# Seven block products for eight in both products of a channel mixing, in two passes through DRAM

## The chip, the cores and the metric

One core of a Trainium2 chip runs the whole program. The metric is the device time of one execution in microseconds (us); the number given for a kernel is the median of several executions. A profile is one further execution with the hardware profiler on; its span runs from the first to the last instruction.

## What is computed

One layer of a decoder trunk, on 2048 prompt tokens and 8 sample tokens, with model width 1024 and float32 inputs and outputs. Token mixing (pooling, gated delta rule and convolution heads) ends in an output projection and a residual, which gives x1. Channel mixing follows. The lines of the reference that matter here are

```
h = rmsnorm(x1) * (1 + scale2) + shift2          # (tokens, 1024)
a = square(relu(h @ w_ff1))                      # w_ff1 (1024, 4096)
x2 = x1 + gate2 * (a @ w_ff2)                    # w_ff2 (4096, 1024)
y = rmsnorm(x2) * g_final
```

in shortened names. The change touches only these lines and the final norm, and leaves token mixing alone.

## The kernel before

All products are made at float32 accuracy out of the faster fp32r format: an operand is kept as a pair, hi (the operand rounded to fp32r, by a cast on ACT) and lo (the operand less hi, by a subtraction in `split_lo`, L125, in channel mixing always on DVE). A product is three matmuls into one PSUM bank: hi by hi, hi by lo, lo by hi. `unit_mm` (L148 to L157) does this for a tile of 128 weight columns over the 8 slices of the 1024 channels.

Token mixing is the program's first part, and its last instructions on PE are the output projection (L156, `ps_ip`), on DVE the residual (L1108, L1109), and on SP the store of x1 to DRAM (L1111, `x_scr`).

Channel mixing (from L1337) runs in two groups of 8 token tiles, the 8 samples being extra columns of the second group. For each group the rows of x1 are loaded (`ff_load`), scaled (L1389), transposed, given scale and shift and split into pairs of 1024 or 1032 columns (`ff_act`, `ff_rows`; PE L184, ACT L189, DVE L193 and L125). Then a loop goes over the 32 tiles of 128 hidden channels:

- `ff1(ft)` loads 128 columns of w_ff1 (`load_unit`, L136) and 128 rows of w_ff2 (L1416), splits both, makes the first product (L156, `ps_f`, blocks of 512 columns in the first group and of 344 in the second), and forms the squared ReLU as a pair: ACT L1423 (ReLU out of PSUM) and L1429 (square), DVE L1430 and L1431.
- `ff2(b, res)` takes a pair of hidden tiles, makes the second product of all 8 token tiles by 2 halves of 512 columns (L1460, 6 matmuls into one bank) and adds it to a sum held in SBUF (DVE L1473; for the first pair ACT L1471).
- For the samples the second product is a small fp32 product (L1441, `ps_smp`, 8 matmuls for a pair of hidden tiles, and DVE L1446).

The first group ends in `finish` (L1487 ff.: gate on POOL, L1496; second residual and final norm on DVE, L1497 and L1501). The second ends in `finish_last` (POOL L1507 and L1526, DVE L1508, L1523, L1524 and L1535, ACT L1533), which takes the last two pairs of hidden tiles product by product. The intermediate, 2048 tokens by 4096 hidden channels, never leaves SBUF.

No table by hand sets the order. The program is written in the order above, and a scheduler in the Tile framework lays out one in-order instruction list for each engine (PE, DVE, ACT, POOL, and SP, which issues the DMAs), from its own estimate of times, from priorities, and from the pools: a tile can be written only when the tile that had its buffer before has been read by all its readers.

## Time and profile before

| | |
|---|---|
| median of 3 runs | 2618.52 us (2617.0 to 2619.83) |
| profiled execution: span | 2612.9 us, mean granted TensorE clock 0.987 |
| median of the runs less that span | 5.6 us |
| busy share of the span | PE 96%, DVE 65%, ACT 36%, POOL 14% |
| DMA | 253.66 MB moved, mean 97 GB/s |

The profiled execution is listed by its span alone; the time of a run also takes in what lies around the span, and that is put at the 5.6 us of the table. Busy is the time in which an engine worked at something. PE's matmuls are pipelined, so that the mean duration of a single one is longer than the distance from one start to the next; the distance is what counts. The chain that ended last is followed back from the last instruction, at each step to what released it.

### The profile page before, as it was taken

Reading aid. Unit: us, or ns where it says so; the run is one execution under the profiler, and the core shown is the slowest. Engines: PE = TensorE matmul, PEld = TensorE weight load, DVE = VectorE, ACT = ScalarE, POOL = GpSimd, SP = SyncE. Lnnn points to the kernel's source line nnn. Section 1 sums busy time; section 2 is a strip of 40 time slices with the busy share of each in tenths; the row PEclk is TensorE's granted clock in tenths of the full one; section 3 lists DMA queues with packets and bytes.
Section 4 is the critical chain, followed back from the end, with each engine's and each line's share of the span. In section 5 each row is a group of like instructions: output and inputs, shape, how many; then the busy total and the mean of one; then the engine's idle time right before and its main releaser. Section 6 shows DMA issues by size and latency. Waiting matters only on the chain.

```text
span 2612.9 us, 35642 instructions
## 1 busy us (share of the span) xinstructions
PE 2512.9 (96%) x13789; PEld 2087.7 (80%) x13789; DVE 1690.0 (65%) x3107; ACT 938.3 (36%) x2021; POOL 355.8 (14%) x257
## 2 busy tenths in 40 slices
PE   7989999989999999999999999999999999999997
PEld 4667777777889788778888888888888888888885
DVE  4978988999898777644444444445854544444458
ACT  3366367348347442552121121212632122121223
POOL 2111212112112235300000000001300000000034
PEclk9999999999999999999999999999999999999998
DMA  8743223323422568741111111112421111111112
GB/s 300 229 142 111 85 77 110 93 81 98 124 87 78 153 213 260 247 140 54 44 49 49 49 49 46 47 37 65 162 81 49 41 50 48 41 49 41 54 43 107
DMA packets 292569, 253.66 MB, mean 97 GB/s; under 512 B 29706, under 2 KB 243403, under 8 KB 292376
## 3 DMA queue, kind: packets, MB, share of 16 engines
q1 hardware_dynamic: 168208, 185.19, 21.9%
q10 hardware_dynamic: 122720, 61.87, 8.5%
q0 software_dynamic: 1472, 4.33, 0.5%
q8 instruction: 108, 1.77, 0.3%
q14 instruction: 61, 0.50, 0.1%
HBM read 218.19 MB, written 33.54 MB: 96 GB/s over the span
## 4 chain that ended last, share of the span: by engine, by line
PE 71%; DVE 18%; DMA 5%; ACT 3%; issue 2%; SPq 0%; POOL 0%; ACTq 0%; DVEq 0%
PE ps_f L156 27%; PE ps_f L1460 26%; PE ps_ip L156 10%; DVE dc L528 4%; DVE wlo L125 2%; DVE cacc L404 2%; PE ps_mod L283 1%; ACT whi L144 1%; DMA g_scr<-ba 1%; PE ps_ip L1163 1%; PE ps_h L184 1%; DMA mraw<-in_w_ada 1%; PE ps_smp L1441 1%; PE ps_pw L501 1%; DMA xt<-x_scr 0%
## 5 line engine op out<-in xcount | busy, mean ns | idle before, releaser
L1460 PE MATMUL ps_f<-w2h,aa 128*128 128x512 f32 x2048 | 654.0, 395 | 0.0
L1473 DVE TENSOR_TENSOR acc<-ps_f,acc 128x512 f32<-128x512 f32 x432 | 298.3, 690 | 264.1 <-PE ps_f L1460 264.1
L1460 PEld LDWEIGHTS ps_f<-w2h,aa 128*128 128x128 f32 x2048 | 384.2, 188 | 96.6 <-issue 6.2
L156 PE MATMUL ps_f<-fhi,whi 128*128 128x344 f32 (+1 forms) x1280 | 449.0, 351 | 1.6 <-ACT fhi L189 0.4
L156 PE MATMUL ps_f<-flo,whi 128*128 128x344 f32 (+1 forms) x1280 | 448.1, 350 | 0.1
L156 PE MATMUL ps_f<-fhi,wlo 128*128 128x344 f32 (+1 forms) x1280 | 446.8, 349 | 0.1
L156 PE MATMUL ps_ip<-hhi,whi 128*128 128x512 f32 (+1 forms) x1112 | 412.7, 372 | 10.0 <-ACT whi L144 4.9
L156 PE MATMUL ps_ip<-hlo,whi 128*128 128x512 f32 (+1 forms) x1112 | 409.6, 369 | 3.9 <-POOL hlo L125 2.8
L156 PE MATMUL ps_ip<-hhi,wlo 128*128 128x512 f32 (+1 forms) x1112 | 409.5, 369 | 1.5 <-DVE wlo L125 1.0
L1460 PE MATMUL ps_f<-w2l,aa 128*128 128x512 f32 x1024 | 404.3, 395 | 0.0
L144 ACT CAST whi<-raw 128x1024 fp32r<-128x1024 f32 x184 | 192.5, 1046 | 336.1 <-PE ps_f L156 194.6
L125 DVE TENSOR_TENSOR wlo<-raw,whi 128x1024 fp32r<-128x1024 f32 x145 | 188.6, 1300 | 128.9 <-ACT whi L144 126.0
L156 PEld LDWEIGHTS ps_f<-fhi,whi 128*128 128x128 f32 x1280 | 240.7, 188 | 32.3 <-issue 5.8
L1433 ACT CAST w2h<-raw 128x1024 fp32r<-128x1024 f32 x64 | 64.4, 1046 | 562.5 <-PE ps_f L1460 553.7
L156 PEld LDWEIGHTS ps_f<-flo,whi 128*128 128x128 f32 x1280 | 240.7, 188 | 24.0 <-DVE flo L125 0.5
L156 PEld LDWEIGHTS ps_f<-fhi,wlo 128*128 128x128 f32 x1280 | 240.3, 188 | 23.5 <-DVE wlo L125 0.3
L156 PEld LDWEIGHTS ps_ip<-hhi,whi 128*128 128x128 f32 x1112 | 212.7, 191 | 52.6 <-ACT whi L144 8.1
L1430 DVE TENSOR_TENSOR sq<-sq 128x344 f32<-128x344 f32 (+1 forms) x160 | 94.5, 591 | 239.2 <-ACT aa L1429 239.0
L156 PEld LDWEIGHTS ps_ip<-hlo,whi 128*128 128x128 f32 x1112 | 212.6, 191 | 39.2 <-POOL hlo L125 4.0
L156 PEld LDWEIGHTS ps_ip<-hhi,wlo 128*128 128x128 f32 x1112 | 212.6, 191 | 37.3 <-issue 3.0
L1460 PEld LDWEIGHTS ps_f<-w2l,aa 128*128 128x128 f32 x1024 | 192.6, 188 | 43.7
L528 DVE SCALAR_TENSOR_TENSOR dc<-glu,dww,dc 128x512 f32<-128x512 f32 x240 | 199.0, 853 | 2.0
(441 smaller groups left out, 2979.5 us busy)
## 6 DMA issues: line engine op xcount, KB each, us to landing
raw<-in_w_ff SPq DMA_DIRECT2D x128, 512.0 KB
raw<-in_w_in ACTq DMA_DIRECT2D x86, 512.0 KB
mraw<-in_w_ada SPq DMA_DIRECT2D x48, 512.0 KB
raw<-y_scr ACTq DMA_DIRECT2D x32, 512.0 KB
xt<-x_scr SPq DMA_DIRECT2D x32, 512.0 KB
xt<-in_x_prompt SPq DMA_DIRECT2D x16, 512.0 KB
xres<-in_x_prompt SPq DMA_DIRECT2D x32, 256.0 KB
x_scr<-xres SPq DMA_DIRECT2D x32, 256.0 KB
```

Source lines behind the costliest of these rows:

```text
L125: eng.tensor_tensor(out=lo, in0=full, in1=hi, op=ALU.subtract)
L144: nc.scalar.copy(out=hi, in_=raw)
L156: nc.tensor.matmul(out=ps, lhsT=a[:, k, :], rhs=b, start=(i == 0), stop=(i == 3 * KT - 1))
L184: nc.tensor.transpose(ps[:, j, :], xt[:, k * P:(k + 1) * P], ident)
L283: nc.tensor.matmul(out=ps[32 * q:32 * q + 32], lhsT=cT[:, k + i, :], rhs=raw[:, i, :], start=(k + i < 4), stop=(k + i >= 4))
L404: nc.vector.scalar_tensor_tensor(out=acc[:, 0:GT], in0=raw[:, j:j + GT], scalar=cw[:, i, j:j + 1], in1=acc[:, 0:GT], op0=ALU.mult, op1=ALU ...
L501: nc.tensor.matmul(out=ps[:, 0:n], lhsT=pww[:, t, mt * P:(mt + 1) * P], rhs=dc[t][:, 0:n], start=(t == 0), stop=(t == 1))
L528: nc.vector.scalar_tensor_tensor(out=d, in0=gt[:, j:j + GT], scalar=dww[:, t, j:j + 1], in1=d, op0=ALU.mult, op1=ALU.add)
L1430: nc.vector.tensor_tensor(out=q, in0=q, in1=q, op=ALU.mult)
L1433: nc.scalar.copy(out=wh, in_=raw)
L1460: nc.tensor.matmul(out=ps, lhsT=a, rhs=w, start=(i == 0), stop=(i == len(terms) - 1))
L1473: nc.vector.tensor_tensor(out=dst, in0=pv, in1=dst, op=ALU.add)
```

## The change

Both products are cut into 2 by 2 blocks, and the eight block products are made as seven, in Winograd's form of Strassen's algorithm: four sums of blocks of the left operand (S1 to S4), four of the right one (T1 to T4), seven products, and sums of these. The sums of operands are made in float32, and each of the seven operands on either side is then split into its hi and lo pair, so a block product is still three matmuls.

Pass 1 (L1590 ff. of the new file) makes the first product and stores its result. For each half of the tokens (`gi`) the normed rows become 28 operand pairs (`x_ops`; 4 channel slices by 7), which fill 28 buffers of 128 by 2 by 512 (`xb` and `xa`). Then 16 pairs of hidden tiles follow. For each, `w1_ops` loads two tiles of w_ff1 and makes 7 operand pairs (4 sums on POOL, 7 casts on ACT, 7 subtractions on DVE); `unit` makes 84 matmuls into 4 banks and joins them by an ACT copy, an ACT ReLU and 5 DVE additions out of PSUM; the first and the last pair of a half use `unit_by_k`, with 7 banks and a loop over the channel slices outside. `a_ops` forms the squared ReLU (one product on POOL, 3 fused instructions on DVE), the four sums of the second product's left operand (POOL), the 7 pairs (ACT and DVE), and stores them in DRAM (`a_scr`, 7 stores of 512 KB, in pieces of 1 KB). The operands of the second half of the tokens are begun during the first (`x_later`, after pairs 3 and 6, by way of DRAM). The samples' first product is now 16 small fp32 matmuls for a pair of hidden tiles (`sample_unit`).

Pass 2 makes the second product: 8 times (`nb`) two pairs of hidden tiles (`q` 0 and 1), and in each 8 steps of two token tiles. `w2_ops` loads two tiles of w_ff2, multiplies them by the gate (POOL, 128 by 1024), makes the sums (4 on POOL) and the 7 pairs. `a_load` brings 1.83 MB of `a_scr` for each step. `block` makes 42 matmuls and adds them to sums that begin as x1 (ACT copy, 6 DVE additions out of PSUM, 3 POOL additions). In the last `nb` each step ends in the final norm (`final`). w_ff2 is read once, where it was read once for each group.

The core of the diff, additions only, with all of `group`, `ff1`, `ff2`, `finish` and `finish_last` removed:

```
+XB = 12
+AO = 4
+WE = 4
+TB = 8
...
+        def split(entry, full):
+            A.copy(out=entry[:, 0, :], in_=full)
+            sub(V, entry[:, 1, :], full, entry[:, 0, :])
...
+        def left_sums(a11, a12, a21, a22, tmp):
+            s1, s2, s3, s4 = (tmp(f"s{i}") for i in range(1, 5))
+            add(Q, s1, a21, a22)
+            sub(Q, s2, s1, a11)
+            sub(Q, s3, a11, a21)
+            sub(Q, s4, a12, s2)
+            return {A11: a11, A12: a12, A22: a22, S1: s1, S2: s2, S3: s3, S4: s4}
+
+        def right_ops(b11, b12, b21, b22, place):
...
+            put(B11, b11)
+            sub(Q, b11, b12, b11)
+            put(B22, b22)
+            sub(Q, b12, b22, b12)
+            sub(Q, b22, b22, b11)
+            put(T2, b22)
+            put(B21, b21)
+            put(T1, b11)
+            put(T3, b12)
+            sub(Q, b21, b21, b22)
+            put(T4, b21)
...
+        def unit(w, x):
+
+            b = {n: bank("ps_" + n) for n in "xyvz"}
+            got = {}
+            for n, ((l, r), name, first, last) in enumerate(PRODUCTS):
+                for j in range(4):
+                    terms(b[name], w[l], x[j][r], j, first and j == 0, last and j == 3)
...
+        def a_ops(gi, p, c):
+
+            Q.tensor_tensor(out=c[0], in0=c[0], in1=c[0], op=ALU.mult)
+            for i in (2, 1, 3):
+                V.scalar_tensor_tensor(out=c[i], in0=c[i], scalar=0.0, in1=c[i], op0=ALU.max, op1=ALU.mult)
+            ops = left_sums(c[0], c[2], c[1], c[3], tmp)
+            for o in LEFT_ORDER:
+                e = ao.tile([P, 4, 2, P], F32R, tag="a", name="ae")
+                full = ops[o].rearrange("p (j t) -> p j t", j=4)
+                A.copy(out=e[:, :, 0, :], in_=full)
+                sub(V, e[:, :, 1, :], full, e[:, :, 0, :])
+                nc.sync.dma_start(out=a_scr[gi][p][:, :, o, :], in_=e.bitcast(F32).rearrange("p j a t -> p j (a t)"))
...
+        RING2 = [(r2, "o")] * 4 + [(ao, "a")] * AO + [(wp, "whi"), (wp, "wlo")] * 2 + [(we, "e")] * WE
...
+            for i in range(2):
+                raw = wp.tile([P, D], F32, tag="raw", name="raw2")
+                nc.sync.dma_start(out=raw, in_=w_ff2[(2 * p + i) * P:(2 * p + i + 1) * P, :])
+                raws.append(raw)
...
+                for raw in raws:
+                    Q.tensor_tensor(out=raw, in0=raw, in1=g2, op=ALU.mult)
+                return right_ops(*(raw[:, s] for raw in raws for s in halves), lambda o: entry(RING2))
...
+            if (gi, j) == tiles[0] and nb + 1 < NB:
+                w_next = [w2_ops(KB * (nb + 1) + q) for q in range(KB)]
+            if (gi, j) == tiles[-1]:
+                w = w_next
+            block(gi, j, w_now, a_now)
```

`V`, `A` and `Q` are DVE, ACT and POOL. The pool `wp` has 2 buffers for `raw`, and RING2 has 16 places, of which one `nb` holds 14.

Three places show how the order moves. The first is POOL in the loop over hidden tiles. Before, its only work there is a small copy for each tile of the second group; in the first group it has nothing between the `a` memset and the sums of `finish`:

```order
L125 TENSOR_TENSOR wlo<-raw,whi 128x1024
L1356 MEMSET a_11373 128x64
L1496 TENSOR_TENSOR acc_11569<-acc_11569,g_11371 128x512 x2
L1496 TENSOR_TENSOR acc_11570<-acc_11570,g_11371 128x512 x2
L1496 TENSOR_TENSOR acc_11571<-acc_11571,g_11371 128x512 x2
```

Now one pair of hidden tiles in pass 1 gives it nine (c is the square, the first four s are the left operand of the second product, the last four those of a later pair's w_ff1):

```order
L1563 TENSOR_TENSOR c_12130<-c_12130 128x512
L1375 TENSOR_TENSOR s_12176<-c_12157,t_12116 128x512
L1378 TENSOR_TENSOR s_12177<-s_12176,c_12130 128x512
L1378 TENSOR_TENSOR s_12178<-c_12130,c_12157 128x512
L1378 TENSOR_TENSOR s_12179<-u_12102,s_12177 128x512
L1375 TENSOR_TENSOR s_12216<-raw 128x512
L1378 TENSOR_TENSOR s_12217<-s_12216,raw 128x512
L1378 TENSOR_TENSOR s_12218<-raw 128x512
L1378 TENSOR_TENSOR s_12219<-raw,s_12217 128x512
```

The nine recur in this order for every pair.

The second place is DVE in the same loop, the end of one pair's list (ae are pairs on the way to `a_scr`, wo pairs of w_ff1; u, c and t hold the sums of products):

```order
L1375 TENSOR_TENSOR c_12157<-ps_v,u_12102 128x512
L1378 TENSOR_TENSOR ae<-c_12130,ae 128x4x128
L1378 TENSOR_TENSOR wo<-raw,wo 128x512
L1565 SCALAR_TENSOR_TENSOR c_12157<-c_12157 128x512
L1375 TENSOR_TENSOR u_12102<-ps_z,u_12102 128x512
L1378 TENSOR_TENSOR wo<-raw,wo 128x512
L1565 SCALAR_TENSOR_TENSOR u_12102<-u_12102 128x512
L1378 TENSOR_TENSOR ae<-s_12177,ae 128x4x128
L1378 TENSOR_TENSOR ae<-s_12176,ae 128x4x128
L1378 TENSOR_TENSOR ae<-u_12102,ae 128x4x128
```

A pair has 22 DVE instructions, 5 of them with an input in PSUM (L1375), 17 with both inputs in SBUF (14 of L1378, 3 of L1565). Before, the matching stretch had the additions out of PSUM of L1473 and the pairs of L125, L1430 and L1431.

The third place is SP where pass 2 goes from one `nb` to the next; `raw_18060` and `raw_18062` are the two w_ff2 tiles of the second pair (`q` 1), `raw_18654` begins the pairs of the `nb` after:

```order
L1663 DMA ai<-a_scr_2_11376 128x768
L1663 DMA ai<-a_scr_3_11377 128x768
L1663 DMA ai<-a_scr_2_11376 128x1024
L1642 DMA raw_18060<-in_w_ff 128x1024
L1663 DMA ai<-a_scr_3_11377 128x1024
L1663 DMA ai<-a_scr_2_11376 128x768
L1663 DMA ai<-a_scr_3_11377 128x768
L1663 DMA ai<-a_scr_2_11376 128x1024
L1663 DMA ai<-a_scr_3_11377 128x1024
L1642 DMA raw_18062<-in_w_ff 128x1024
L1642 DMA raw_18654<-in_w_ff 128x1024
```

The load of `raw_18062` comes behind four loads for the second step of the new `nb`, which take the buffers that the last step of the old one reads. Before, the loads of w_ff2 (L1416) and w_ff1 (L136) alternated on SP with nothing else.

## Rows read from the trace of the kernel before

**Rows 1.** The span in 40 equal slices: busy tenths of the engines, and what the DMA moved.

```profile
PE   7989999989999999999999999999999999999997
...
DVE  4978988999898777644444444445854544444458
...
POOL 2111212112112235300000000001300000000034
...
GB/s 300 229 142 111 85 77 110 93 81 98 124 87 78 153 213 260 247 140 54 44 49 49 49 49 46 47 37 65 162 81 49 41 50 48 41 49 41 54 43 107
```

**Rows 2.** Busy time by stretch: length, PE, PEld, DVE, ACT, POOL (instructions), granted clock, DMA share, GB/s.

```profile
1125.00:1850.00 725.00, 725.00 (x3157) 587.96 (x3156) 344.19 (x476) 174.32 (x245) 25.75 (x18) 1.00 0.18 56
1850.00:2613.00 763.00, 742.45 (x4085) 652.42 (x4083) 410.40 (x729) 194.16 (x356) 63.45 (x59) 0.99 0.19 63
1000.00:1060.00 60.00, 54.72 (x307) 41.29 (x306) 45.14 (x73) 17.75 (x42) 41.19 (x28) 0.98 0.91 288
```

**Rows 3.** The chain that ended last, in order of time, at channel mixing's start: start, us, what.

```profile
1099.55 5.34 DMA xt<-x_scr
...
1106.99 1.06 ACT xt L1389
...
1122.83 1.84 DMA x_scr<-xres
1124.67 22.52 PE ps_f L156 x96
```

**Rows 4.** The same chain where the second group begins.

```profile
1850.69 1.76 PE ps_h L184 x16
...
1857.21 3.50 DMA xt<-x_scr
...
1863.30 1.20 DVE xt L1497 x2
...
1868.80 18.09 PE ps_f L156 x113
1886.89 0.57 PE ps_smp L1441 x8
...
1919.15 11.55 PE ps_f L156 x72
```

**Rows 5.** Groups of PE matmuls in channel mixing: shapes xcount, busy us, mean ns, idle before.

```profile
L1460 PE MATMUL ps_f<-w2h,aa 128*128 128x512 f32 x2048 | 654.0, 395 | 0.0
L1460 PE MATMUL ps_f<-w2l,aa 128*128 128x512 f32 x1024 | 404.3, 395 | 0.0
```

**Rows 6.** PE in order of time, the last matmul of the program.

```profile
2593.61 0.39 PE L1460 MATMUL ps_f<-w2h,aa 128*128 128x512 f32 x1
```

**Rows 7.** POOL and DVE in order of time, in token mixing's last stretch.

```profile
1095.91 2.64 POOL L125 TENSOR_TENSOR wlo<-raw,whi 128x1024 fp32r<-128x1024 f32 x1 [18.13 <-ACT whi L144]
...
1096.22 2.88 DVE L1109 TENSOR_TENSOR xres<-xres,gated 128x512 f32<-128x512 f32 x1
```

**Rows 8.** Groups of POOL instructions in the whole span.

```profile
L1496 POOL TENSOR_TENSOR acc<-acc,g 128x512 f32<-128x512 f32 x16 | 25.5, 1621 | 693.6 <-DVE acc L1495 693.6
...
L1507 POOL TENSOR_TENSOR acc<-acc,g 128x1024 f32<-128x1024 f32 x8 | 20.1, 2515 | 12.8 <-DVE acc L1473 12.8
...
L847 POOL TENSOR_TENSOR q<-q,fr_y 128x512 f32<-128x512 f32 x16 | 19.7, 1253 | 69.2 <-DVE fr_y L117 42.6 <-DVE xs_y L117 15.0 <-ACT halo_q L402 11.6
```

**Rows 9.** Groups of DVE and ACT instructions in channel mixing.

```profile
L1473 DVE TENSOR_TENSOR acc<-ps_f,acc 128x512 f32<-128x512 f32 x432 | 298.3, 690 | 264.1 <-PE ps_f L1460 264.1
...
L1431 DVE TENSOR_TENSOR aa<-sq,aa 128x512 fp32r<-128x512 f32 x64 | 45.1, 705 | 1.6
...
L1501 DVE SCALAR_TENSOR_TENSOR xt<-xt,nr_y,gf 128x512 f32<-128x512 f32 x16 | 11.2, 743 | 0.0
...
L1495 DVE TENSOR_TENSOR acc<-ps_f,acc 128x512 f32<-128x512 f32 x16 | 10.6, 679 | 0.7 <-PE ps_f L1460 0.7
...
L1471 ACT COPY acc<-ps_f 128x512 f32<-128x512 f32 x32 | 18.2, 587 | 15.3 <-PE ps_f L1460 15.3
```

More of the change, by code (lines that the diff above doesn't have):

```diff
@@ L1338, in hybrid_trunk @@
     wq[0] = nc.sync
[L1339 to L1340 removed]
     NF = DFF // P
[L1342 to L1357 removed]
+    NP = NF // 2
@@ new lines, in hybrid_trunk, with w2_ops @@
+        halves = (slice(0, 512), slice(512, 1024))
+        ph3.close()
+        r2 = ph2.enter_context(tc.tile_pool(name="r2", bufs=4))
+        ai = ph2.enter_context(tc.tile_pool(name="ai", bufs=2 * KB))
+        RING2 = [(r2, "o")] * 4 + [(ao, "a")] * AO + [(wp, "whi"), (wp, "wlo")] * 2 + [(we, "e")] * WE
+        ring[0] = 0
+        def w2_ops(p):
+            raws = []
+            for i in range(2):
+                raw = wp.tile([P, D], F32, tag="raw", name="raw2")
+                nc.sync.dma_start(out=raw, in_=w_ff2[(2 * p + i) * P:(2 * p + i + 1) * P, :])
+                raws.append(raw)
+            Q.tensor_copy(out=a32[:, p % 2, :, 0:NS], in_=a_s[:, 2 * p:2 * p + 2, :])
+            ps = bank("ps_s3", psa)[:, 0:256]
+            for j in range(4):
+                for i in range(2):
+                    nc.tensor.matmul(out=ps[32 * j:32 * j + 32], lhsT=a32[:, p % 2, i, :], rhs=raws[i][:, 256 * j:256 * j + 256],
+                                     start=(i == 0), stop=(i == 1))
+            if p == 0:
+                A.copy(out=chunks, in_=ps)
+            else:
+                add(V, chunks, ps, chunks)
+            with tc.high_priority(offset=HP):
+                for raw in raws:
+                    Q.tensor_tensor(out=raw, in0=raw, in1=g2, op=ALU.mult)
+                return right_ops(*(raw[:, s] for raw in raws for s in halves), lambda o: entry(RING2))
@@ new lines, in a_load, with x1_load @@
+        def a_load(gi, j, p):
+            tiles = []
+            for o, n in ((0, 4), (4, 3)):
+                e = ai.tile([P, n, 2, P], F32R, tag=f"i{n}", name="ai")
+                nc.sync.dma_start(out=e.bitcast(F32).rearrange("p o a t -> p o (a t)"), in_=a_scr[gi][p][:, j, o:o + n, :])
+                tiles.append(e)
+            return tiles
+        acc = {}
+        def x1_load(gi, j):
+            for th in range(2):
+                t = 8 * gi + 4 * th + j
+                acc[t] = xa.tile([P, D], F32, tag="x", name="acc")
+                load_rows(x1_scr[t * P:(t + 1) * P, :], P, acc[t])
@@ new lines, in block @@
+        def block(gi, j, w, a):
+            b = {n: bank("ps_" + n) for n in "xyvz"}
+            t1, t2 = 8 * gi + j, 8 * gi + 4 + j
+            c11, c12, c21, c22 = acc[t1][:, halves[0]], acc[t1][:, halves[1]], acc[t2][:, halves[0]], acc[t2][:, halves[1]]
+            for n, ((l, r), name, first, last) in enumerate(PRODUCTS):
+                ps = b[name]
+                for q in range(KB):
+                    at_ = a[q][l // 4][:, l % 4]
+                    for i, (x, y) in enumerate(PAIRS):
+                        nc.tensor.matmul(out=ps, lhsT=at_[:, x, :], rhs=w[q][r][:, y, :],
+                                         start=first and q == 0 and i == 0, stop=last and q == KB - 1 and i == 2,
+                                         skip_group_check=True)
+                if n == 0:
+                    s = tmp("s")
+                    A.copy(out=s, in_=ps)
+                elif n == 1:
+                    u2 = tmp("u2")
+                    add(V, u2, ps, s)
+                    add(Q, c12, c12, u2)
+                    add(Q, c21, c21, u2)
+                elif n == 2:
+                    add(V, s, ps, u2)
+                    add(Q, c22, c22, s)
+                elif n == 3:
+                    add(V, c11, ps, c11)
+                elif n == 4:
+                    add(V, c22, ps, c22)
+                elif n == 5:
+                    add(V, c12, ps, c12)
+                else:
+                    add(V, c21, ps, c21)
@@ L1584 @@
     from concourse.bass_utils import run_bass_kernel_spmd
-    nc = bacc.Bacc("TRN2", target_bir_lowering=False, num_devices=1)
+    nc = bacc.Bacc("TRN2", target_bir_lowering=False, num_devices=1, dynamic_dma_scratch_size=2048)
     arrays, args = {}, []
```

444 lines of the change are left out of this document (243 added, 201 removed).

## The prediction, made before the changed kernel was run

> **What bounds the kernel now.** I read the span in slices first [rows 1]: PE is at nine tenths in nearly every slice, and in the channel mixing (from about slice 18) DVE stands at four to five tenths, POOL at nothing but for the change of groups and the end, and the DMA moves some 50 GB/s. The busy times by stretch say the same [rows 2]: 725.00 of 725 us of PE up to 1850, 742.45 of 763 after it, at a granted clock of 1.00 and 0.99. So PE's matmuls set the time there, and every other engine has room. The chain of waits gives the pace [rows 3, 4]: 96 matmuls of 512 columns in 22.52 us, 72 of 344 in 11.55. One matmul's record is 0.39 us long [rows 6], about 0.16 more than the distance of two starts, so the distance is (22.52-0.16)/96 = 0.233 us, and 0.158 for 344 columns. The same chain shows where the channel mixing begins on PE (1124.67, [rows 3]), the program's last matmul ends at 2594.0 [rows 6], and 18.9 us of norm follow.
>
> **What goes.** The first product has 1536 matmuls of 512 columns and 2304 of 344, the second 2048 + 1024 [rows 5] of 512: 1536 x 0.233 + 2304 x 0.158 + 3072 x 0.233 = 1438 us. The change makes 2688 of 512 for each product, 5376 x 0.233 = 1253 us. PE is relieved of 185 us. The samples' 32 groups of 0.57 us in the second product [rows 4] stay, 18 us. If PE stayed the bound and nothing waited, the end would come about 185 us earlier. The question is how much of it the new work of DVE, POOL and the queues takes back.
>
> **DVE against POOL, the largest term.** Until now POOL hardly works beside DVE. Where it does, the trace shows what happens [rows 7]: a POOL subtraction runs from 1095.91 to 1098.55; a DVE addition with both inputs in SBUF starts at 1096.22 and is done only at 1099.10, 0.55 us after POOL's end. Alone, such DVE instructions take 0.60 us each back to back (two in 1.20, [rows 4]). It works the other way as well: POOL's 512-column product takes 1253 ns in one place and 1621 in the stretch where DVE works between [rows 8]. DVE additions with an input in PSUM, in that same stretch, stay at 679 ns, as everywhere else at 690 [rows 9]. So the two take turns, save for DVE's additions out of PSUM.
>
> A pair of hidden tiles in pass 1 has 9 POOL instructions and 17 of DVE with both inputs in SBUF. In turns they take 9 x 1.253 = 11.3, plus 9 x 0.55 behind POOL, plus 8 x 0.60 behind DVE, together 21.0 us. PE's 84 matmuls take 19.6. So PE is no longer the bound there. DVE works in order: near a pair's end four stores' subtractions (the ae rows) stand behind the last fused square, which waits for PE's last product, and two of the POOL sums for these. I add 1.3 us for what of that hole the five additions out of PSUM don't fill, and take 22.3 us. Ends: 19.6 (the turns hidden) and 21.0 + 5 x 0.68 = 24.4 (nothing of the additions hidden). 32 x 22.3 = 714 us. ACT has some 16 instructions of 0.59 [rows 9], 9.4 us, and is hidden.
>
> The Trainium skill, page "SBUF — State Buffer", section "Who interferes with whom", speaks against this change: a VectorE instruction with two SBUF inputs contends with a GpSimd instruction that reads SBUF, whoever is first keeps the port for the whole instruction, and the other is fully blocked, while one SBUF input doesn't contend. The trace agrees (0.55 us after POOL's end; 679 ns undisturbed). By that rule a pair costs 21.0 us at least, without it 19.6: 45 us over 32 pairs.
>
> **The stages of pass 1.** Making 28 pairs of the normed rows takes 16 POOL sums and 28 DVE subtractions, in turns 16 x 1.253 + 28 x 0.60 = 36.8 us. At the start, the second four row tiles are loaded only behind the last store of x1, which lands at 1124.67 [rows 3]: 5.3 us for loads in a row and 1.1 for the scale [rows 3], then 36.8, then the last fourth of PE's first unit (4.9), less the 22.3 that this pair has in the sum already: 26 us (10 to 40). At the change of halves the 28 buffers come free a fourth at a time during the last unit; three fourths of 36.8 and 4.9 lie open: 33 us (15 to 45). `x_later` adds 64 transposes at 0.11 [rows 4], 7 us. The sample products of pass 1 are on PE, which has 2.7 us to spare in each pair: nothing; without that cover 16 x 18 small matmuls of at most 0.07 (8 in 0.57, [rows 4]), 20 us.
>
> **To pass 2.** Its buffers take the place of those of the x operands, so the first loads wait for the last unit: 1.83 MB at 288 GB/s, the best stretch seen [rows 2], 6.4 us, then two POOL products of 2.5 [rows 8], two sums of 1.25, cast and subtraction 1.2, of which only some overlap: 15 us. The nearest stall of this kind, at the change of groups, is 11.6 us from load to the next run of matmuls [rows 4]; ends 8 and 25.
>
> **Pass 2.** 2688 x 0.233 = 626 us and 18 for samples. A step takes PE 9.8 us; its 6 DVE additions (4.1), 3 POOL sums (3.8, in no turn with these) and 1.83 MB of loads (6.4) lie beside it: nothing; without that cover a step would be the sum of a load and its products. At each of the 7 changes of `nb` there is something open. Of 16 ring places 14 are held, and `raw` has 2 buffers, so the second pair's tiles are loaded only when the first pair is split, which waits for the old step's last products. On SP `raw_18062` stands behind four loads that wait for the same step. It lands at 2.35 MB/288 = 8.1 us (alone 3.5, [rows 4]); two products, two sums, cast and subtraction make its T2 ready at 16.8. Meanwhile PE has 33 matmuls of the first pair and the samples, 8.3. Open: 8.5 us each, 60 us (27 with the load alone; 98 at 14 each, if the first pair's five late splits come in turns with POOL too). On POOL the steps' sums queue behind the gate products, on DVE behind the late splits; PE then has 5 banks for 4 in use.
>
> The last `nb` adds 4 fused products of 0.74 [rows 9] and a short chain for every step; its 9.6 us on DVE about fill the step: 4 us (0 to 8). After the last matmul one addition, square sums, the chain, four products and a store (1.84, [rows 3]) make 10 us in place of 18.9.
>
> **Sum.** 1124.7 + 714 + 26 + 33 + 7 + 15 + 626 + 18 + 60 + 4 + 10 = 2638 us of span, against 2612.9: 25 us more. What lies around the span is 5.6 us by the median of the runs, so 2643 us: **slower by about 1%**. By parts: 185 of matmuls, about 13 of the old change of groups (1469 less 1438 and 18) and 9 of the tail go; pass 1's turns bring 87, its stages 66, pass 2's changes 79.
>
> **Rivals.**
> - *The turns don't bind* (faster): DVE and POOL meet less than I think, and PE sets pass 1. Then 32 x 19.6 = 627 with 20 for samples; the start falls to 12, the change to 16 (20 us of POOL sums in place of 36.8 in turns); the sum is 1124.7 + 647 + 12 + 16 + 7 + 15 + 626 + 18 + 60 + 4 + 10 = 2540, time 2545. For it: my 21.0 is near 19.6, and the additions out of PSUM fit under POOL. Against: rows 7 and 8. It decides from 21.5 us for a pair: 0.8 us less in each of 32 undoes the 25 us.
> - *The changes of `nb` run in series* (slower): 17 us in place of 8.5 at each of the 7, when the five late splits hold up ACT and DVE and no bank is free for the first pair's work: 60 more, 2703. For it: the SP order. Against: PE's order has work of the first pair ahead of the second's.
> - *The stores bind*: 3.67 MB stored and 1.05 loaded in 22.3 us is 212 GB/s, against 288 seen [rows 2], and four buffers for seven stores of 3.5 us [rows 4] pass in 8 us. Only at under three fourths of the rate seen does this bind; at half of it a pair would take 33 us and the time be some 340 us longer. The Trainium skill, page "Perfetto Trace Analysis", section "DMA Optimizations", warns of transfers under 2 KB, and the stores are in pieces of 1 KB; no row here times such stores by themselves.
> - *It doesn't do what it says*: the lists of instructions hold 84 matmuls for a pair in place of 96, so no.
>
> **How the numbers follow.** A measurement of this kernel can tell about 0.2%, 5 us, from no change. The forecast, from 2600 to 2690, gets 0.46; the first rival, 2500 to 2600, 0.35; the second, over 2690, 0.16; the third 0.03. Of the forecast's part 0.06 lies below 2613 and 0.05 within 5 us of no change. So faster 0.41, same 0.05, slower 0.54. The range goes from 2540, just under the first rival's time, to 2740, the second rival's 2703 with the upper ends of start, change of halves and change of passes on top (14 + 12 + 10); about 1 in 10 is left out at either end.
>
> **What would show it.** Pass 1: PE busy about 85 to 90% of the stretch, the distance of two pairs 22 us, DVE's ae and wo subtractions with a mean well over 0.7 us, POOL's sums over 1.25, the squares and sums of DVE out of PSUM still 0.68. A distance of 19.6 and a PE strip of nines makes the first rival right. Pass 2: seven gaps of PE of 6 to 11 us, each ended by a w_ff2 pair, and none in the steps between. PE's matmul time must fall by 185 us; if it doesn't, the clock was lower or the pace not 0.233, and the whole sum is wrong.

## The result, and the profile after

The changed kernel takes 2831.94 us (median of 4 runs, 2829.26 to 2839.94) against 2619.18: a ratio of 1.081, 95% interval 1.080 to 1.083. It is slower by 8.1%, where about 1% was forecast and the range ended at 2740. The profiled execution spans 2827.3 us, 214 more than before and 190 more than the sum's 2638.

The page of the changed kernel, busy time and the strips that answer to [rows 1], with the busy time of before ahead of it:

```profile
PE 2512.9 (96%) x13789; PEld 2087.7 (80%) x13789; DVE 1690.0 (65%) x3107; ACT 938.3 (36%) x2021; POOL 355.8 (14%) x257
```
```profile
PE 2480.7 (88%) x12797; PEld 1925.3 (68%) x12797; DVE 2094.4 (74%) x3369; ACT 1027.7 (36%) x2252; POOL 1199.1 (42%) x808
...
PE   7989998999999997799898799995888978978976
...
DVE  4988998999987766699899899995444544544467
...
POOL 2111221222122362556566666563654554555442
PEclk9999999999999999899999899997999988988978
...
GB/s 301 228 112 104 96 78 99 95 90 120 91 78 156 223 263 186 77 230 252 245 219 187 164 212 206 202 200 334 139 167 171 171 145 168 176 160 155 201 124 167
```

PE's nines are broken from slice 16 on. In pass 1 (slices 16 to 27) DVE stands at eight to nine for most of it and POOL at five to six; in pass 2 no engine is full, and PE's strip goes up and down. PE's busy time fell by 32 us where the sum took 185 of matmuls away: that is one of the prediction's own signs of being wrong, and a lower clock is one of the two reasons that it names for it. The pattern of pass 2 is one that no term of the sum had at this size. The busy times by stage, to be read with [rows 2] (length, PE, PEld, DVE, ACT, POOL, clock, DMA share, GB/s), say how much:

```profile
1125.00:1935.00 810.00, 711.70 (x3363) 548.69 (x3364) 712.76 (x797) 342.29 (x598) 488.33 (x313) 0.94 0.63 203
1935.00:2070.00 135.00, 93.67 (x386) 67.97 (x384) 68.05 (x84) 21.71 (x37) 71.69 (x50) 0.82 0.62 219
2070.00:2680.00 610.00, 537.49 (x2210) 397.27 (x2209) 290.45 (x386) 78.38 (x132) 320.57 (x227) 0.91 0.48 166
2680.00:2827.00 147.00, 97.60 (x352) 68.87 (x352) 94.55 (x200) 31.49 (x83) 43.97 (x31) 0.84 0.44 154
```

The rows are pass 1, the boundary with the first `nb`, six `nb` in the middle, and the last with the end. Set against the sum, stage by stage (us). An `nb` is counted from its first product to the next one's; by the sum it takes (626 + 18)/8 = 80.5 without a change. The last product of pass 1 ends at 1935.4, the first `nb` begins at 1939.6, the second at 2070.1, the last at 2680.0, and the last product of all ends at 2816.5.

| stage | sum | measured | difference |
|---|---|---|---|
| pass 1, 1124.7 to its last product | 780 | 811 | +31 |
| boundary (last product of pass 1 to the second `nb`, less 80.5) | 15 | 54 | +39 |
| seven changes of `nb`, each | 8.5 | 21.1 | +88 |
| last `nb`, less 80.5 and a change | 4 | 35 | +31 |
| after the last product | 10 | 11 | +1 |

That is the whole 190.

The rows also say what a change's 21.1 us are made of. In the six middle `nb` PE is idle for (610 - 537.49)/6 = 12.1 us of each, where the sum had 8.5. The other 9 are busy time: 537.49/6 = 89.6 us for 80.5 by the sum. Part of that is the clock. In these 610 us PE was granted the lower of its two levels (1.2 GHz) for 106 us and was busy in 72 of them; there one product starts 0.427 us after the other (2289.26 and 2289.68, for example), at the higher level (2.4 GHz) 0.231. By these numbers 33 us of the six `nb`, 5.5 of each, are products at the lower level; this is an estimate. The sum had no term for it. The same estimate gives 30 us of PE's time in pass 1 (where DVE is the fuller engine, so not all of it lengthens the span), 8 at the boundary and 12 in the last `nb`.

What happens at a change shows in the chain of waits of the changed kernel, from 2268 (start, us, what):

```profile
2268.23 5.84 DMA raw<-in_w_ff
2274.07 0.02 issue
2274.09 0.04 POOLq L1656
2274.14 8.81 issue
2282.95 0.04 POOLq L1656
2282.99 4.66 POOL raw L1656 x2
...
2288.32 6.84 DVE wo L1378 x4
```

The first of the second pair's two tiles lands at 2274, 3.4 us after the new `nb`'s first product (2270.74). But the gate product that should follow begins 8.8 us later. It writes over the tile, and the samples' product, which reads both tiles, must come first. PE in order of time shows what that one waits for (in brackets, idle time before and what ended it):

```profile
2270.74 0.97 PE L1685 MATMUL ps_x<-wo,ai 128*128 128x512 f32 x3
2271.54 0.87 PE L1685 MATMUL ps_y<-wo,ai 128*128 128x512 f32 x3
2272.24 0.85 PE L1685 MATMUL ps_v<-wo,ai 128*128 128x512 f32 x3
2272.94 0.85 PE L1685 MATMUL ps_z<-wo,ai 128*128 128x512 f32 x3
2274.20 0.59 PE L1648 MATMUL ps_s<-raw,a 128*32 128x256 f32 x2 [0.42 <-DMA raw<-in_w_ff]
2278.59 1.48 PE L1685 MATMUL ps_x<-wo,ai 128*128 128x512 f32 x3 [3.79 <-DMA ai<-a_scr]
2280.93 1.95 PE L1648 MATMUL ps_s<-raw,a 128*32 128x256 f32 x14 [0.86 <-DMA raw<-in_w_ff]
2286.03 1.22 PE L1685 MATMUL ps_x<-wo,ai 128*128 128x512 f32 x2 [3.15 <-ACT wo L1381]
```

The second tile, which SP issues behind five `a_scr` loads, lands at 2280.89, and the rest of the samples' product begins 0.04 us later. It is so in all seven changes: the second tile lands 7.3 to 10.2 us after the `nb`'s first product (9.0 in the mean), PE stands idle for it for 0.8 to 1.5 us, and the samples' product begins within 0.05 us of it. Its place in PE's list, behind three products that wait for an `a_scr` load, costs nothing beyond that as long as the second tile comes last. In all seven changes PE has 15 products of the first pair before it waits for the second pair's first operand. PE's own waits over three changes (us, times, longest):

```profile
PE ps_x L1685 <- DMA ai<-a_scr: 14.2, 10, 3.8
PE ps_x L1685 <- ACT wo L1381: 9.4, 3, 3.1
PE ps_s L1648 <- DMA raw<-in_w_ff: 4.9, 5, 1.5
```

SP's issues, in order of time (start, us), and under them its longest wait for a buffer of `a_scr` loads in the same stretch (us, times, longest):

```profile
2268.65 2.77 SPq L1663 DMA_DIRECT2D ai<-a_scr  x5
2271.51 25.83 SPq L1642 DMA_DIRECT2D raw<-in_w_ff  x3
2304.42 6.68 SPq L1663 DMA_DIRECT2D ai<-a_scr  x8
```
```profile
SPq L1663 <- PE ps_v L1685: 9.3, 5, 7.0
```

The three loads of w_ff2 are the second tile, which goes out at once, and the two of the `nb` after, which hold SP to 2297 because the two `raw` buffers are not free. But that hold isn't what makes the next `a_scr` loads late: when it ends, SP waits 7.0 us more, until PE has read the buffer that the first of them takes (4.3 to 8.3 us in the six middle changes). After the waits at a change PE works at a lower clock: 0.73 from 2275 to 2300, where it was 1.00 in the 15 us before.

### The profile page after: what moved, and what is told of

Same layout as the page of the kernel before. It is cut to its first block, busy times and chain, and to the rows that moved or that the text cites. A ratio compares the mean times of both kernels' runs of the same rounds, so it can differ in the third digit from the quotient of the medians.

```text
span 2827.3 us, 36365 instructions
## 1 busy us (share of the span) xinstructions
PE 2480.7 (88%) x12797; PEld 1925.3 (68%) x12797; DVE 2094.4 (74%) x3369; ACT 1027.7 (36%) x2252; POOL 1199.1 (42%) x808
## 4 chain that ended last, share of the span: by engine, by line
PE 37%; DVE 28%; DMA 11%; issue 11%; POOL 7%; ACT 5%; SPq 1%; ACTq 0%; DVEq 0%; POOLq 0%
PE ps_ip L160 11%; PE ps_x L1685 5%; DVE wo L1378 5%; DVE ae L1378 5%; PE ps_v L1685 5%; PE ps_z L1685 4%; DMA ai<-a_scr 3%; DVE dc L532 3%; PE ps_y L1685 2%; DMA raw<-in_w_ff 2%; POOL s L1378 2%; DVE cacc L408 1%; DVE wlo L129 1%; POOL raw L1656 1%; POOL s L1375 1%
## 5 line engine op out<-in xcount | busy, mean ns | idle before, releaser
L1685 PE MATMUL ps_x<-wo,ai 128*128 128x512 f32 x768 | 238.7, 447 | 97.0 <-DMA ai<-a_scr 45.7
L1375 POOL TENSOR_TENSOR acc<-acc,u 128x512 f32<-128x512 f32 x128 | 169.1, 1344 | 284.0 <-DVE u L1375 215.0
L1685 PEld LDWEIGHTS ps_x<-wo,ai 128*128 128x128 f32 x768 | 154.1, 211 | 169.3 <-ACT wo L1381 35.8
L1378 DVE TENSOR_TENSOR wo<-raw,wo 128x512 fp32r<-128x512 f32 x208 | 234.1, 1136 | 47.1 <-ACT wo L1381 44.5
L1685 PE MATMUL ps_v<-wo,ai 128*128 128x512 f32 x768 | 207.0, 402 | 16.3 <-ACT wo L1381 12.9
L1685 PE MATMUL ps_z<-wo,ai 128*128 128x512 f32 x768 | 203.9, 404 | 13.8 <-DVE acc L1375 9.1
L1378 DVE TENSOR_TENSOR ae<-s,ae 128x512 fp32r<-128x512 f32 x132 | 180.0, 1381 | 32.3 <-ACT ae L1570 30.5
L1508 PE MATMUL ps_v<-xo,wo 128*128 128x512 f32 x672 | 175.0, 411 | 21.8 <-DVE t L1375 21.8
L1685 PEld LDWEIGHTS ps_v<-wo,ai 128*128 128x128 f32 x768 | 146.0, 192 | 56.9 <-ACT wo L1381 13.6
L1508 PE MATMUL ps_x<-xo,wo 128*128 128x512 f32 x672 | 174.1, 409 | 8.3 <-ACT s L1520 6.6
L1375 DVE TENSOR_TENSOR u<-ps_y,s 128x512 f32<-128x512 f32 x92 | 62.7, 685 | 148.5 <-ACT s L1690 117.3
```

The source lines that it names most:

```text
L1375: eng.tensor_tensor(out=out, in0=in0, in1=in1, op=ALU.add)
L1378: eng.tensor_tensor(out=out, in0=in0, in1=in1, op=ALU.subtract)
L1508: nc.tensor.matmul(out=ps, lhsT=w[:, a, c], rhs=x[:, b, :], start=start and i == 0, stop=stop and i == 2, skip_group_check=True)
L1685: nc.tensor.matmul(out=ps, lhsT=at_[:, x, :], rhs=w[q][r][:, y, :], start=first and q == 0 and i == 0, stop=last and q == KB - 1 and i == ...
```

## The experiments

All times are spans of single profiled runs, to be compared with 2827.3; the changed kernel's own four runs have 2827.3 to 2838.0, so what a single edit does is read from its stage rather than from the span. "Pair" is the mean of the 13 distances, in each half, of the copies that open a pair's joining (ACT L1520); for the changed kernel 22.8 us in the first half and 23.3 in the second. One `nb` is the mean of the six in the middle, 101.7 us (101.0 to 102.4 in the six other runs that leave pass 2's middle alone).

**The arithmetic of pass 1 on DVE** (`dve_p1`): POOL's sums and squares change engine.

```
-            add(Q, s1, a21, a22)
+            add(V, s1, a21, a22)
...
-            Q.tensor_tensor(out=c[0], in0=c[0], in1=c[0], op=ALU.mult)
+            V.tensor_tensor(out=c[0], in0=c[0], in1=c[0], op=ALU.mult)
```

> All POOL sums and squares of pass 1 (9 for a pair of hidden tiles, and the 32 sums of the x operands) go to DVE, which nobody then takes turns with. Theory of the turns: DVE has 31 instructions for a pair, 26 x 0.60 + 5 x 0.68 = 19.0 us, under PE's 19.6, so the distance of two pairs falls from the 21 to 22.5 us of the changed kernel to 20.5 or less, and start and change of halves lose some 8 us each; the span falls from 2827 by 50 to 80 us. Rival, order and dependences within a pair set it: DVE is longer by 9 x 0.6 = 5.4 us in a chain that already decides, so the distance stays at 22 or grows and the span is the same or up to 100 us longer.

Measured: 2809.9. Pairs 23.6 and 23.2, no shorter. The change of halves is 18 us shorter. The second pair's first copy comes at 1194.9 instead of 1200.6, which says little: runs with pass 1 untouched have it anywhere from 1200.6 to 1208.0. The turns themselves went: DVE's subtraction for a stored operand, in the changed kernel and then here,

```profile
L1378 DVE TENSOR_TENSOR ae<-s,ae 128x512 fp32r<-128x512 f32 x44 | 62.0, 1429 | 6.3 <-ACT ae L1570 5.5
```
```profile
L1378 DVE TENSOR_TENSOR ae<-s,ae 128x512 fp32r<-128x512 f32 x44 | 29.4, 684 | 0.5 <-ACT ae L1570 0.5
```

falls from 1429 to 684 ns, but DVE has nine more instructions to a pair. Over the same 250 us, in the changed kernel and then here (length, PE, PEld, DVE, ACT, POOL, clock, DMA share, GB/s):

```profile
1630.00:1880.00 250.00, 234.67 (x1278) 177.89 (x1277) 230.90 (x262) 100.42 (x183) 149.94 (x96) 0.99 0.65 204
```
```profile
1630.00:1880.00 250.00, 234.32 (x1271) 178.08 (x1272) 208.03 (x357) 102.81 (x184) 0.00 (x0) 0.99 0.64 204
```

DVE is busy for 23 us less, and the pairs are no shorter. So the turns are real, and moving the work is no cure. Whether they set the pair this run can't tell.

**The sums left out** (`no_sums`): the eight POOL sums of a pair go and nothing takes their place.

```
-            add(Q, s1, a21, a22)
-            sub(Q, s2, s1, a11)
-            sub(Q, s3, a11, a21)
-            sub(Q, s4, a12, s2)
+            s1, s2, s3, s4 = a21, a22, a11, a12
```

> Leaves out the eight POOL sums of a pair in pass 1 (the sums S1 to S4 are replaced by unsummed blocks, so every product but two has a wrong operand); DVE, ACT, matmuls, stores and loads of a pair stay as they are, POOL keeps one square. Theory that taking turns with POOL (and waiting for its sums) sets a pair: the distance falls from 21.1 (first half, pairs without extra work) and 23.3 (second half) to 19.5 to 20 and 21 to 21.5, as in the run that made the weight operands once. Rival, DVE's list by itself does, since moving the sums to DVE changed nothing: the distance stays within 0.7 us.

Measured: 2721.1, pairs 19.8 and 21.2, with PE busy all the time:

```profile
1630.00:1800.00 170.00, 170.00 (x949) 132.82 (x948) 114.25 (x194) 77.58 (x138) 8.33 (x8) 1.00 0.70 224
```

In the changed kernel it was busy for 234.67 of 250 us from 1630 on. DVE has the same 22 instructions to a pair as there. So POOL's sums set the pair. Whether they do it by the turns, by the wait for them or by the buffers that they hold, which go with them here, this run doesn't separate.

**The weight operands made once** (`w_once`), in both passes.

```
-                    w = w1_ops(raws)
+                    if gi == 0 and p == 0:
+                        w = w1_ops(raws)
...
-                w_next = [w2_ops(KB * (nb + 1) + q) for q in range(KB)]
+                w_next = w
```

> Leaves out the making of weight operands after the first: pass 1 uses the first pair's seven w_ff1 operands for all 32 pairs, pass 2 the first nb's for all 8 (so most products are of the wrong weights); the loads of w_ff1, the matmuls, the stores and the additions stay. In pass 1 DVE loses 7 of 22 instructions and POOL 4 of 9 for a pair. Theory that the making of operands, in turns and in DVE's order, sets a pair: the distance falls from 22.5 us (gi 1: 23.3) to 20 to 20.7 (gi 1: 21.5, with 1.35 for the samples). Rival, the tail of a pair (squares, sums and stores) sets it: 22 or more. In pass 2 nothing is made at a change: one nb falls from 101.7 us to 78.3 to 80, the steps alone; if more is left, the a_scr loads or the additions bind, and the span says how much.

Measured: 2578.6. Pairs 19.3 and 20.5, below the expectation; one `nb` 80.5, a little over it: the steps alone, without the samples' products and the loads of w_ff2, which go with the operands in pass 2. The boundary is at 56 us (54 in the changed kernel), and the last `nb` keeps 30 of its 35. Even with seven eighths of the matmuls and next to no weight operands to make, the program is only 34 us shorter than before.

**The order of DVE's list in pass 1** (`psum_first`): additions out of PSUM ahead of the next weights.

```
+                hpx = tc.high_priority(offset=PSP)
+                hpx.__enter__()
                 if n == 0:
```

> In pass 1 the instructions that read a pair's products out of PSUM get a higher priority than the making of the next weight pairs; the amount of work is the same. Theory that the order of DVE's list sets a pair (PE waits for two of these additions, about 2.7 us in 22.5): the mean distance of two pairs falls to 20.5 to 21.5 us, pass 1 by 30 to 60 us. Rival, DVE and POOL in turns are full: what the additions gain the weight pairs lose, the distance stays within 0.5 us of 22.5.

Measured: 2833.1, pairs 22.6 and 22.7. The rival held: what the additions gain the rest loses.

**Four buffers for w_ff2** (`raw4`).

```
-                raw = wp.tile([P, D], F32, tag="raw", name="raw2")
+                raw = xpool.tile([P, D], F32, tag="x", name="raw2") if p % 2 else wp.tile([P, D], F32, tag="raw", name="raw2")
```

> The two w_ff2 tiles of the second pair of each nb come into two other buffers, so that four are there instead of two and SP no longer waits with them; nothing else changes. Theory of the queues: the second pair's tiles are there long before the change, SP doesn't hold the a_scr loads behind them, and each of the 7 changes loses 8 to 12 us; the span falls by 55 to 85 us. Rival, what follows the load (gate product, sums and subtractions in turns, ring places) sets the change: under 25 us less.

Measured: 2725.9, one `nb` 87.3. More than the expectation's upper end: 14.4 us of a change's 21.1 go with the two buffers, some 9 of them idle time of PE and 5 busy time. In its trace SP's three loads take 4.94 us in place of 25.83:

```profile
2249.44 4.94 SPq L1642 DMA_DIRECT2D raw<-in_w_ff  x3
2258.56 62.38 SPq L1663 DMA_DIRECT2D ai<-a_scr  x26
```

and PE's waits for `a_scr` loads over a stretch as long as above fall from 14.2 us to 5.2:

```profile
PE ps_x L1685 <- DMA ai<-a_scr: 5.2, 8, 1.4
```

Its clock over the six middle `nb` is 0.99, where the changed kernel had 0.91.

**The gate product in tiles of its own** (`gate_wt`), so that it needn't wait for the samples' product.

```
-                for raw in raws:
-                    Q.tensor_tensor(out=raw, in0=raw, in1=g2, op=ALU.mult)
+                        ws.append(wtmp("gated"))
+                        Q.tensor_tensor(out=ws[-1], in0=raw[:, s], in1=g2[:, s], op=ALU.mult)
```

> The gate product of w_ff2 is written into four separate tiles of 512 columns instead of over the loaded tile, so that it needn't wait for the sample product in PE's order, and the loaded tile is free after both; POOL has four products of 1.25 in place of two of 2.4. Theory that PE's order holds the chain (tiles landed at 2274, gate product begun at 2283 in the changed kernel): up to 9 us less at each change, the span 35 to 65 us shorter. Rival, the loads of a_scr and the chain in turns set it: within 15 us of the changed kernel.

Measured: 2747.7, one `nb` 90.8: 10.9 us a change, and again more than expected. The run changes two things at once: the gate product of the first tile needn't wait for the samples' product, and so not for the second tile either, and the loaded tiles come free earlier, so that later loads go out earlier. What the wait for the samples' product costs by itself it doesn't give.

**POOL's DMA queue for w_ff2** (`raw_poolq`): two buffers as before, but SP free.

```
-                nc.sync.dma_start(out=raw, in_=w_ff2[(2 * p + i) * P:(2 * p + i + 1) * P, :])
+                nc.gpsimd.dma_start(out=raw, in_=w_ff2[(2 * p + i) * P:(2 * p + i + 1) * P, :])
```

> The w_ff2 loads go to POOL's DMA queue, so that SP never holds a_scr loads behind them; the two buffers and so the lateness of the second pair's load stay as in the changed kernel. Theory that the hold on SP is the main cost of a change: one nb falls from 101.7 us by 6 or more. Rival, the late load is: under 3 us less, or more, since POOL's additions now wait behind the load's wait.

Measured: 2843.0, one `nb` 102.8. The hold on SP is in plain view in the trace, but without it nothing is won as long as the tile comes late, as the 7.0 us that SP waits behind the hold let one expect. (POOL's additions now stand behind that wait, which this run can't separate.)

**Pass 2's arithmetic on DVE** (`dve_p2`), POOL's `Q` to `V` in the gate product, the sums of w_ff2 and the three additions of a step.

> All POOL arithmetic of pass 2 (gate products, sums of w_ff2, three additions of a step) goes to DVE; pass 1 as in the changed kernel. Theory of the turns in pass 2: at a change of nb the two gate products fall from 4.7 to about 2.4 us, three sums from 4.6 to 1.8, five subtractions from 9.1 to about 3.5; the open time of each of the 7 changes falls from about 20 us by 8 or more, the span by 60 or more. Rival, the queues (raw and a_scr loads, the sample product in PE's order) set the changes: under 25 us less. If neither, the steps themselves become longer, since DVE has 9 instructions for 9.8 us of PE.

Measured: 2778.0, one `nb` 94.8: 6.9 us a change, 48 for seven, and the span is 49 us shorter. Between the two theories: turns cost there, but less than the lateness.

**The three together** (`p2_free`: four buffers, gate product in four separate tiles, all on DVE).

> Pass 2 with four buffers for w_ff2 tiles, gate products into separate tiles, and all of its arithmetic on DVE; pass 1 untouched. One nb takes 101.7 us on average in the changed kernel, 87.3 with four buffers alone, 90.8 with the separate gate product alone, 94.8 with DVE alone; its matmuls and samples are 80.6. Theory that the three costs share one late chain (load, then gate product, then turns): once the load is early the others matter little, and one nb stays at 84 to 87, the span at 2700 to 2727. Rival, they add: one nb at 81 to 82, the span near 2685.

Measured: 2764.4, one `nb` 93.6. Both expectations failed; it is slower than four buffers alone. PE's waits over three changes were

```profile
PE ps_x L1688 <- DMA ai<-a_scr: 13.8, 14, 4.5
PE ps_s L1648 <- DMA raw<-in_w_ff: 8.1, 2, 4.8
```

so transfers are late again; over the same three changes SP's loads of w_ff2 wait 32.9 us for gate products. A likely reason, not tried, is that four separate tiles hold one pair only, so the second pair waits for the first's splits once more.

**Boundary and last `nb`** (`ends`): two edits in two stages.

```
-                e = ao.tile([P, 4, 2, P], F32R, tag="a", name="ae")
+                e = xa.tile([P, 4, 2, P], F32R, tag="x", name="ae") if own else ao.tile([P, 4, 2, P], F32R, tag="a", name="ae")
...
+                if due:
+                    final(due)
+                due = [(acc[t], P, y_prompt[0, t * P:(t + 1) * P, :]) for t in (8 * gi + j, 8 * gi + 4 + j)]
```

> Two edits in two places, read apart by stage: the final norm of a step is written behind the next step's products, and the seven operand pairs that the last pair of pass 1 stores get buffers of their own. Theory: in the last nb (136.5 us from its first product to the end in the changed kernel, 80.6 of matmuls) DVE's norm work stands ahead of the next step's additions, so it falls by 15 to 30 us; at the passes' boundary the last subtractions wait for stores that land after 9.5 and 10.2 us behind a_scr loads, so the time from pass 1's last product to the second nb (134.6 us) falls by 10 to 20. Rival for the first: the square sums on ACT and the chain of small instructions are as long as a step, so under 8 us; for the second: gate product and turns set it, under 5 us.

Measured: 2808.8. The last `nb` falls from 136.5 to 116.3 us: the norm work stood ahead of the next step's additions, 20 of its 35 us. In the changed kernel PE and DVE wait there as follows:

```profile
PE ps_z L1685 <- DVE acc L1375: 9.1, 5, 6.3
```
```profile
DVE sq L1375 <- ACT junk L1710: 10.2, 7, 1.5
```

The boundary doesn't move (136.6 us from pass 1's last product to the second `nb`, 134.7 in the changed kernel): waiting for the stores isn't what holds it.

**The last pair's work left out** (`tail_skip`; the pair before is stored in its place).

```
-                a_ops(gi, p, c)
+                if not (gi == 1 and p == NP - 1):
+                    a_ops(gi, p, c)
```

> Leaves out squares, sums, splits and stores of the very last pair of pass 1 (the pair before is stored twice in its place, so one pair's share of the second product is wrong). Theory that at the boundary the last pair's work on POOL, DVE and ACT stands before the making of the first w_ff2 operands: the first nb, from its first product to the next, falls from 130.5 us by 10 to 15. Rival, the gate products and sums of w_ff2 alone set it, or the wait for the buffers of the x operands: under 5 us less.

Measured: 2829.4; the first `nb` 126.8 for 130.5. PE now waits in one place:

```profile
PE ps_s L1650 <- DMA raw<-in_w_ff: 21.5, 1, 21.5
```

the second pair's tiles, which SP issues behind 14 loads of x1 and the first pair's splits.

**That and four buffers** (`tail_raw4`).

> The last pair's squares, sums, splits and stores left out (as in the run before that did so) and four buffers for w_ff2 tiles, together. The first nb took 130.5 us in the changed kernel, 126.8 without the last pair's work, 124 with four buffers; each by itself leaves the other in the way (the second pair's load, 21.5 us of PE's wait without the last pair's work; ACT's casts behind stores with four buffers). Theory that these two are alternatives in parallel: together the first nb falls to 95 to 108 us. Rival, the chain of gate products and sums sets the boundary: 118 or more.

Measured: 2713.8; the first `nb` 105.0, where four buffers alone give 124.0. By themselves the two edits bring 6.5 and 3.7 us, together 25.5: two waits side by side, of which either hides the other. (The first `nb` has 130.5 to 132.5 in the three kernels that leave the boundary as it is, so 3.7 by itself is not far above the spread.) That leaves 30 us of the boundary's 54, which no run took apart; in this trace PE still waits there 9.2 us for one cast of a w_ff2 operand and 7.4 for `a_scr` loads.

**The start** (`start_x`): the second pair's w_ff1 tiles in other buffers.

```
+                if loads[0] in (2, 3):
+                    raw = xpool.tile([P, KT, P], F32, tag="x", name="raw1")
```

> The two w_ff1 tiles of the second pair of pass 1 come into other buffers, which are free some 20 us earlier, and stand on SP ahead of four row loads that they stood behind. Theory that this late load holds up the second pair (its copy out of PSUM is at 1200.6 us in the changed kernel, where my sum had about 1176): it comes 12 to 20 us earlier. Rival, the x operands, in turns on DVE and POOL, set the start: under 5 us.

Measured: 2829.6; the tiles land at 1160 instead of 1187, and the second pair's copy comes at 1207.7, within the 1200.6 to 1208.0 of runs with pass 1 untouched. My theory fell, though that load stands on the chain of the changed kernel (1181.01, 4.04 us). The only run that moved it clearly is the one without POOL's sums of a pair, to 1187.5: POOL's work, beside that for the x operands, is in the way there.

**What could be joined.** `combo` has the edits of `p2_free`, `ends` and `psum_first`, and the x operands' sums on DVE; `best` has four buffers, the later norm, the x sums on DVE and a fifth buffer for stored operands.

```
-AO = 4
+AO = 5
```

> All edits of the three kernels above together, with the sums of the x operands on DVE besides. By stage: pass 1 some 25 us shorter for the x sums (start 6, change of halves 18 in the run with all sums on DVE) and 0 to 60 for the order, the boundary 10 to 20, the seven changes 100 to 140, the last nb 15 to 30. Together 2570 to 2680 us. Rival, the stages share one cost, so that half of it comes back elsewhere: over 2680.

> Four buffers for w_ff2 tiles, the norm of a step behind the next step's products, the sums of the x operands on DVE, and a fifth buffer for stored operands, which is a third spare place in pass 2's ring. From the single edits: 2726 less 10 to 20 for the last nb, 20 to 25 for start and change of halves, 0 to 20 for the fifth buffer: 2660 to 2700 us, still slower than before by 2 to 3%. Rival, the four edits reach below 2640.

Measured: `combo` 2704.9, with one `nb` at 93.0 (over the expectation's 2680). `best` 2715.5, also over its expectation, by its 2 runs 2720.98 us, 1.038 times before (interval 1.034 to 1.042). Neither beats the kernel before. The fifth buffer brought nothing: one `nb` is at 89.2.

## Why the prediction was wrong

**Right: the direction, the number of matmuls, the mean of the pairs.** 5376 products are recorded, and at the higher clock level they start 0.231 us apart. A pair was put at 22.3 us; without the two that carry `x_later`, the first half has 21.1 and the second 23.3, a mean of 22.3 over 24 distances. That the mean agrees so well is luck: the first half is 1.2 under the sum, and the second is lifted by the samples, which had been put at nothing. The direction of the reason holds: without POOL's sums a pair falls to 19.8 and 21.2 (`no_sums`), and DVE's subtraction takes 1429 ns beside a busy POOL and 684 with POOL idle. That the pair is long by the turns alone, as the prediction had it, isn't shown: `dve_p1` took the turns away and not the work, and the pairs stayed. The Trainium skill's rule (page "SBUF — State Buffer", section "Who interferes with whom") agrees with these rows: the same subtraction is back at 684 ns once POOL is idle. The first rival, with PE as the bound, was wrong, and so was the one on stores at a low rate: without the sums a pair goes at PE's pace while the DMA moves 224 GB/s.

**Wrong: "Pass 2", the change of `nb`** (8.5 us taken, 14 as the high end, 21.1 measured; 88 of the 190). The step that failed is "Meanwhile PE has 33 matmuls of the first pair and the samples, 8.3". PE had 15 products of the first pair, 3.5 us, and the last three of these waited for an `a_scr` load. The samples were no cover: they need both tiles, so they waited for the second one (2280.89, by the sum 2278.8), and the gate product, which the sum begins with the landing, waited for them. I had asked what is behind a waiting instruction on POOL and DVE, not what PE's own filling work waits for. So PE stood idle 12.1 us in place of 8.5. The rest of the 21.1 is a term that the sum didn't have: it took every product at 0.233 us, and behind these waits PE ran at the lower clock level, by the estimate above 5.5 us of each change. Some 3.5 us of busy time stay unexplained; `raw4` has them too (504.91/6 = 84.2 at a clock of 0.99). Having the tiles early gives back 14.4 us (`raw4`), tiles of its own for the gate product 10.9 (`gate_wt`). The second rival named the place and 17 us, for another reason (late splits, no free bank); it had 0.16.

**Wrong: "To pass 2", the boundary** (15 us, ends 8 and 25; 54 measured). I priced the way to one operand. By `tail_raw4` two waits lie side by side there, the last pair's own work and the second pair's late load, worth 25 us together and 6.5 and 3.7 by themselves; the remaining 30 stays open.

**Wrong: the last `nb`** (4 us, ends 0 and 8; 35). I set DVE's 9.6 us against a step of 9.8 and took that for cover. But DVE works in order, and the norm waits for square sums on ACT with the next step's additions behind it; `ends` got 20 us back by order alone. The other 15 no run took apart.

**Wrong: "The stages of pass 1"** (+31). The second pair's first copy is due at 1124.7 + 26 + 22.3 + 2.8 = 1175.8 by the sum and comes at 1200.6, 25 us later. From there to the end of pass 1 only 6 more are lost: the change of halves is 9 us longer than taken, the two pairs with `x_later` stand 22 us above their neighbours, where 7 was taken, and other pairs are shorter. Of the start, the making of the x operands is the term that failed in plain view: by the sum the last of the 28 is ready at 1124.7 + 5.3 + 1.1 + 36.8 = 1167.9, in the trace at 1184.5, of which the loads are 5 us and the making itself 12 (48.5 for 36.8). `start_x` shows that the late w_ff1 load isn't the cause; what the rest is stays open, beyond POOL's share (`no_sums`). "The sample products of pass 1 ... nothing" was wrong as well: the second half's pairs are 2.2 us longer than the first's, and still 1.4 longer when POOL's sums are gone (21.2 and 19.8, the latter with `x_later` in it).

All four have one thing in common: I multiplied durations and hid them under an engine with time to spare, in a stage with no steady state, and I priced waits without the slower clock behind them. The 24 steady distances came out right in the mean; the transitions, each priced by one chain, came out at 1.3 (the change of halves) to nine times their price.

## What to carry to other kernels

Where a change replaces work of the busiest engine by more work on the others, price the transitions first: for each load or operand that becomes due there, write down every reader that must be done before its buffer or its overwriting is free, with its place in its own in-order list and what it waits for itself. A small product that nobody seems to wait for becomes a gate when its operand is overwritten in place: here it needed two tiles, and so held the work on the first until the second had landed. After the change, compare busy time with the sum as well as waits: nearly half of a change's cost stood in PE's busy time. When two edits each gain almost nothing at a stall, try both together before naming a third cause.

## What the runs showed of the hardware

- The granted clock at a change: 1.00 from 2260 to 2275, and 0.73 from 2275 to 2300, a stretch that holds PE's waits of 3.8 and 3.2 us; over the six middle `nb` 0.91 in the changed kernel and 0.99 with four buffers (`raw4`). At the lower level (1.2 GHz) products of 512 columns start 0.427 us apart, at the higher (2.4 GHz) 0.231.

```profile
2260.00:2275.00 15.00, 14.28 (x60) 10.59 (x58) 9.21 (x13) 2.67 (x5) 7.23 (x6) 1.00 0.59 190
2275.00:2300.00 25.00, 14.52 (x49) 8.15 (x50) 13.12 (x12) 5.20 (x9) 13.00 (x9) 0.73 0.31 114
```
```profile
2071.00:2595.00 524.00, 504.91 (x2209) 382.39 (x2208) 287.56 (x385) 78.00 (x133) 319.44 (x227) 0.99 0.55 194
```

- A 512 KB store that is issued behind `a_scr` loads landed 9.5 us after its issue, the one before them after 4.3:

```profile
1926.64 4.26 DMA a_scr<-ae
...
1934.54 9.53 DMA a_scr<-ae
```
